# Expert 0 of a mixture of experts: 64 columns as column-tiled F32 pairs in place of 128 columns as split weights

## The chip, the cores and the metric

One core of one Trainium2 chip runs the whole program. The metric is device time in microseconds (us) of one execution; the median of several runs is compared. PE is the matrix engine, PEld its weight load, ACT the scalar engine, DVE the vector engine, POOL the general one, SP the engine that issues nearly all loads here.

## What is computed

A two-layer generator over 256 latent tokens and 256 context tokens, width 1024, all in float32. Each layer mixes tokens with three head groups (gated linear attention, differential softmax attention, neighbourhood attention); layer 0 then has a dense SwiGLU of 2816, layer 1 a mixture of eight experts:

```python
def moe_swiglu(h, w_router, wg, wu, wd):
    logits = (t @ w_router).astype(jnp.float32)
    top_v, top_i = lax.top_k(logits, TOP_K)          # 2 of 8
    top_w = jax.nn.softmax(top_v, axis=-1)
    gates = jnp.sum(jax.nn.one_hot(top_i, N_EXPERTS) * top_w[..., None], axis=1)
    for e in range(N_EXPERTS):
        y = y + gates[:, e:e + 1] * swiglu(t, wg[e], wu[e], wd[e])   # (silu(t wg) * (t wu)) wd
```

An expert's three matrices are 1024 x 3584, 1024 x 3584 and 3584 x 1024, 44.04 MB in all; the eight are 352.3 MB. In layer 1 only the 256 latent tokens pass the experts, 512 token-expert pairs. For the inputs of `setup_inputs()` the router gives the experts 60, 76, 99, 60, 73, 57, 35 and 52 tokens; expert 0 has the first figure.

## The kernel before

Layer 0, then layer 1's mixer with its output projection (four weight tiles, `m2` = 0 to 3, the last matmuls are named `psw`), then the norm, the router, and the experts. An expert works only on its own tokens: one-hot matrices `S` are built from positions (`onehots`), a matmul with `S` gathers the tokens (`gather`, tiles `pga`), and one with its transpose scatters the result back into `xtk` (`scatter_half`, tiles `py`).

Which expert is worked in which place is decided on the chip: `order_experts` sums the tokens per expert (`pcnt`), ranks the experts and permutes positions and gates; `order_index` gives the ranks as integers (`ordi`); `load_order` reads seven of them into SP's registers, since SP addresses the weights of places 1 to 7 by them. Expert 0 is always in place 0 and needs none of it, so that its weights can be loaded ahead.

- Places 0 to 3 are **big**: up to 128 tokens, `expert()`. The hidden 3584 are taken in seven blocks `j` of 512 columns. A block loads two tiles each of gate, up and down, 1.049 MB each, 42 loads an expert. To keep float32 precision every tile is split: ACT rounds it (`eh`, line 804), DVE takes the rest (`el`, line 805), and PE makes three products (lines 151 to 153, and 1151 for down).
- Places 4 to 7 are **small**: up to 64 tokens, `expert_small()`. Weights are used as plain F32, with nothing to split: gate fills PSUM partitions 0 to 63 and up 64 to 127, as a pair (`pgs`, line 1280; `pds` is the down projection, line 1265). Four blocks `j` of 896 columns, each with eight loads of 0.918 MB and four of down (three of 1.049, one of 0.524 MB), 48 loads an expert.

If an expert exceeds its cap, a loop behind a branch (`cv > 0`) runs over all eight experts in two blocks of 128 tokens each, as big experts.

Loads go through a ring of SBUF slots: `slot32(i)` gives load number `i` the next name, and SP's DMA waits until the slot's last reader is done (for a big tile the reader that ends last is `el`). `first` lists the slots of the first 13 loads, `ring` the rest, and `until` the load from which a slot is needed for something else; big experts have ten slots at first, seven from load 42 and five from load 62. `prefetch(i)` issues loads 0 and 1 and their split inside the output projection (`m2` = 1 and 3).

Work that lies between the experts' matmuls is hung on blocks by `plan`: key `(place, j)`, functions run after that block. `add_x` brings the residual stream into `xtk` by 16 transposes (`pxt`). `FILLS` spreads chunks of the modulation vectors (`mod_cols`, 16 matmuls `psmod` and two transposes `ptmod` each) over the earlier stages; its fourth entry stands for the gap at the norm between layer 0's channel mixer and layer 1's mixer. A scheduler then interleaves each engine's instructions, so neighbouring steps of the code mix.

## Time and profile before

| | |
|---|---|
| median of 3 runs | 1952.09 us (1951.88 to 1953.65) |
| profiled execution | 1952.91 us, span 1951.1 us |
| granted PE clock, mean | 0.985 of full speed |
| PE busy | 1814.2 us, 93% |
| DVE, ACT busy | 979.4 us, 758.6 us |
| DMA | 480.05 MB, mean 246 GB/s |
| chain that ended last | PE 72%, DMA 16%, DVE 7%, ACT 3% |

The span is the stretch of the profile from the first to the last instruction; the execution's own time is 1.8 us longer. The page's 40 slices are of 48.8 us. The experts begin in slice 20 and take up the second half of the program; 352.3 of the 480 MB are moved there.

### The profile page before, as it was taken

To read this page: it belongs to the slowest core of one execution; us is meant where nothing else is said; L and a number is where in the kernel's file an instruction comes from. 1 tells how busy PE (TensorE), PEld (TensorE's weight loads), DVE (VectorE), ACT (ScalarE), POOL (GpSimd) and SP (SyncE) were. 2 spreads that over 40 slices of the span, in tenths; PEclk is the share of its full clock that TensorE was granted. 3 is DMA by queue.
4 is the path that set the end of the run, shared out by engine and by line. 5 is a ranking of instruction groups with operands and counts; after the bars stand their busy time and mean duration, and the time that the engine had idled before them with its cause. 6 is when DMAs were issued, how large, how long until landed. Compare 5 with 4: busy or idle time off the path is not lost.

```text
span 1951.1 us, 23538 instructions
## 1 busy us (share of the span) xinstructions
PE 1814.2 (93%) x9280; PEld 1267.4 (65%) x9280; DVE 979.4 (50%) x1294; ACT 758.6 (39%) x965; POOL 46.6 (2%) x75
## 2 busy tenths in 40 slices
PE   7998999999999998999999999999999988787886
PEld 4755766778887876767778778888786333232332
DVE  5474555533333345765669788888985201010101
ACT  4424455422212224344657677767664100000001
POOL 1030000000000000120000000000000000000000
PEclk9999999999999999999989999999999899999999
DMA  9665232343234244564289798999998999999996
GB/s 287 224 179 146 71 129 88 99 145 106 82 108 151 87 132 136 162 161 141 66 306 355 264 320 316 353 327 354 350 353 321 394 410 411 410 410 409 410 410 258
DMA packets 255778, 480.05 MB, mean 246 GB/s; under 512 B 11630, under 2 KB 141996, under 8 KB 249516
## 3 DMA queue, kind: packets, MB, share of 16 engines
q1 hardware_dynamic: 253152, 474.19, 67.8%
q0 software_dynamic: 1312, 2.62, 0.9%
q8 instruction: 75, 1.23, 0.3%
q10 hardware_dynamic: 1196, 1.66, 0.3%
q14 instruction: 43, 0.35, 0.0%
HBM read 477.39 MB, written 1.05 MB: 245 GB/s over the span
## 4 chain that ended last, share of the span: by engine, by line
PE 72%; DMA 16%; DVE 7%; ACT 3%; issue 2%; SPq 0%; POOL 0%; DVEq 0%; ACTq 0%; POOLq 0%
DMA e<-in_w_moe_up_dram 11%; PE pd L1151 8%; PE pgs L1280 3%; DMA e<-in_w_moe_down_dram 3%; PE pu L152 3%; PE pg L151 3%; PE pu L153 3%; PE pg L152 3%; PE pu L151 3%; PE pg L153 3%; PE pds L1265 2%; PE psg L151 2%; PE psg L152 2%; PE psg L153 2%; PE psu L152 2%; PE psu L151 2%
## 5 line engine op out<-in xcount | busy, mean ns | idle before, releaser
L805 DVE TENSOR_TENSOR el<-e,eh 128x2048 fp32r<-128x2048 f32 (+1 forms) x173 | 375.5, 2190 | 50.5 <-ACT eh L804 49.7
L804 ACT ACTIVATE eh<-e 128x2048 fp32r<-128x2048 f32 (+1 forms) x173 | 316.7, 1838 | 94.1 <-PE pu L153 31.8
L1280 PE MATMUL pgs<-e,xs 128*64 128x448 f32 x1024 | 222.8, 552 | 51.3 <-DMA e<-in_w_moe_up_dram 51.3
L144 ACT ACTIVATE wh<-w 128x2048 fp32r<-128x2048 f32 (+2 forms) x70 | 125.3, 1791 | 208.4 <-issue 80.0
L1280 PEld LDWEIGHTS pgs<-e,xs 128*64 128x64 f32 x1024 | 75.1, 138 | 191.9 <-issue 98.7
L145 DVE TENSOR_TENSOR wl<-w,wh 128x2048 fp32r<-128x2048 f32 (+2 forms) x70 | 149.7, 2138 | 98.3 <-ACT wh L144 98.3
L1291 DVE TENSOR_TENSOR es<-es,pgs 64x448 f32<-64x448 f32 x32 | 19.9, 622 | 297.9 <-ACT es L1290 297.9
L1290 ACT ACTIVATE es<-pgs 64x448 f32<-64x448 f32 x32 | 17.2, 537 | 300.6 <-PE pgs L1280 290.3
L1265 PE MATMUL pds<-e,gts 128*64 128x512 f32 x448 | 111.4, 606 | 2.5 <-DMA e<-in_w_moe_down_dram 1.7
L151 PE MATMUL pg<-eh,xeH 128*128 128x512 f32 x224 | 89.9, 402 | 0.6 <-ACT eh L804 0.6
L152 PE MATMUL pg<-el,xeH 128*128 128x512 f32 x224 | 90.0, 402 | 0.0
L151 PE MATMUL psp<-hH,wh 128*128 128x512 f32 (+1 forms) x224 | 86.4, 388 | 3.4 <-ACT hH L276 3.3
L153 PE MATMUL pg<-eh,xeL 128*128 128x512 f32 x224 | 88.9, 397 | 0.0
L152 PE MATMUL pu<-el,xeH 128*128 128x512 f32 x224 | 88.2, 394 | 0.7 <-DVE el L805 0.6
L151 PE MATMUL pu<-eh,xeH 128*128 128x512 f32 x224 | 88.8, 396 | 0.0
L151 PE MATMUL psq<-wh,hH 128*128 128x256 f32 x304 | 88.4, 291 | 0.0
L153 PE MATMUL pu<-eh,xeL 128*128 128x512 f32 x224 | 87.7, 391 | 0.0
L152 PE MATMUL psq<-wl,hH 128*128 128x256 f32 x304 | 87.6, 288 | 0.0
L153 PE MATMUL psq<-wh,hL 128*128 128x256 f32 x304 | 87.3, 287 | 0.0
L152 PE MATMUL psp<-hL,wh 128*128 128x512 f32 (+1 forms) x224 | 85.6, 382 | 0.0
L153 PE MATMUL psp<-hH,wl 128*128 128x512 f32 (+1 forms) x224 | 85.2, 381 | 0.0
L1151 PE MATMUL pd<-eh,gth 128*128 128x512 f32 x224 | 71.2, 400 | 2.6 <-ACT eh L804 2.4
(504 smaller groups left out, 3445.8 us busy)
## 6 DMA issues: line engine op xcount, KB each, us to landing
...
```

Source lines behind the costliest of these rows:

```text
L144: act(wh[:, :m], w32[:, :m], AF.Copy)
L145: tt(wl[:, :m], w32[:, :m], f32(wh[:, :m]), ALU.subtract)
L151: mm(ps, lhsT=sh, rhs=mh, start=first, stop=False)
L152: mm(ps, lhsT=sh, rhs=ml, start=False, stop=False)
L153: mm(ps, lhsT=sl, rhs=mh, start=False, stop=last)
L804: act(h3[:, b], w[:, b], AF.Copy)
L805: tt(l3[:, b], w[:, b], f32(h3[:, b]), ALU.subtract)
L1151: mm(pds[o], lhsT=gt[sh][:, q, :], rhs=w[mh][:, k, o * 512:(o + 1) * 512], start=a and j == 0 and q == 0, stop=z and j == NJ - 1 and q == 3)
L1265: mm(pd[0][H * o:H * o + H, :], lhsT=gt[:, q, :], rhs=w[:, k, o * 512:(o + 1) * 512], start=j == 0 and q == 0, stop=j == NB - 1 and q == F ...
L1280: mm(ps[H * o:H * o + H, b, 0:HB], lhsT=xv[:, kk, :], rhs=ws[o][:, k, b * HB:(b + 1) * HB], start=kk == 0, stop=kk == KD - 1, skip_group_c ...
L1290: act(gv, ps[0:H, b, 0:HB], AF.Silu)
L1291: tt(gv, gv, ps[H:P, b, 0:HB], ALU.mult)
```

## The change

Expert 0, in place 0, is worked as a small expert.

- `CAPS` and the new `SMALL` give place 0 a cap of 64. Its 64 gathered columns `x0` lie in the free half of `xT`, and its tail is that of a small expert.
- `prefetch()` runs once, at `m2` = 3, and issues seven plain loads (`EARLY`) without a split; eight more ring slots follow (`w` to `y`), 15 in all. `until` takes `xt` away at load 24, `mh`, `ml`, `ch` and `cl` at load 30 (big experts need them for split weights), `xh` and `xl` at 68 and `y` at 84. The slot `xc` is gone; `xm` joins the ring after block 0 of place 3, not after block 0 of place 4.
- `plan` has the order of the experts one block earlier, `load_order` with it; `add_x` and the gather of place 1 after block 2 of place 0. `add_x` now copies, since it writes `xtk` first, and the scatter of place 0 adds.
- Every split is one ACT and one DVE instruction (before, the first eight tiles had two).
- `FILLS`: one chunk earlier in layer 0, and two chunks of the layer-1 vectors in the norm gap. `scores()` puts both query tiles of a context head into one bank (layer 0 only).

```diff
@@ -28,12 +28,14 @@
 NE = 8
 EPS = 1e-6
 PRI = 1
-FILLS = "21011010111002110010110011100|11|11100021101|00|2101101110212121110|2".split("|")
-PF = (1, 3)
+FILLS = "21011010111101110010110011100|11|11100021101|11|2101101110111121110|2".split("|")
+NFIRST = 100
+EARLY = ["r0", "r1", "r2", "mh", "ml", "mh", "ml"]
 NBIG = 4
+SMALL = (0, 4, 5, 6, 7)
 FB = 896
 FK = FB // 128
-CAPS = [P] * NBIG + [P // 2] * (NE - NBIG)
+CAPS = [P // 2 if e in SMALL else P for e in range(NE)]
...
     def scores(name, q, k, W, q0, k0):
-        ps = [bank(psc, name) for _ in range(2)]
-        for m in range(2):
-            r = slice(64 * m, 64 * m + 64)
-            mm(ps[m][:, :W], lhsT=q[r, q0:q0 + P], rhs=k[r, k0:k0 + W], start=True, stop=True)
-        return ps
+        n = NT // W
+        while True:
+            ps = [bank(psc, name) for _ in range(2)]
+            for i in range(n):
+                for m in range(2):
+                    r = slice(64 * m, 64 * m + 64)
+                    mm(ps[m][:, i * W:(i + 1) * W], lhsT=q[r, q0:q0 + P], rhs=k[r, k0:k0 + W], start=True, stop=True)
+                q0 += P
+            for i in range(n):
+                yield [p[:, i * W:(i + 1) * W] for p in ps]
...
+                    ps = next(pairs)
...
-            if l == 1 and m2 in PF:
-                prefetch(PF.index(m2))
+            if l == 1 and m2 == 3:
+                prefetch()
...
     def convert(i, w32, dram, kk, n, pl):
...
-        w = w32 if len(w32.shape) == 3 else w32.rearrange("p (b n) -> p b n", n=256)
-        if len(w32.shape) == 3:
...
-        else:
-            nc.sync.dma_start(w32.rearrange("p (k n) -> p k n", n=n), dram)
-        st = 4 if i < 8 else (2 if i in (NE * 42 - 2, NE * 42 - 1) else 8)
+        w = w32.rearrange("p (b n) -> p b n", n=256)
+        nc.sync.dma_start(w32.rearrange("p (k n) -> p k n", n=n), dram)
+        st = 8
         h3 = wh.rearrange("p (b n) -> p b n", n=256)
         l3 = wl.rearrange("p (b n) -> p b n", n=256)
...
-    def prefetch(i):
+    def gu_cols(w_ap, c, j):
+        return w_ap[c * 256:(c + 1) * 256, j * FB:(j + 1) * FB].rearrange("(k p) n -> p k n", p=P)
+
+    def prefetch():
         nonlocal mpr
-        if i == 0:
-            mpr = pool("mpr", 2, side="right")
-        ready[i] = convert(i, ring_tile(f"r{i}"), wm_g[0, 0, i * 512:(i + 1) * 512, 0:512].rearrange("(k p) n -> p k n", p=P), 4, 512, mpr)
+        mpr = pool("mpr", 2, side="right")
+        for i, nm in enumerate(EARLY):
+            w32 = ring_tile(nm) if nm[0] == "r" else mpr.tile([P, 2048], F32, tag="w" + nm[1], name="e32")
+            nc.sync.dma_start(w32[:, :2 * FB].rearrange("p (k n) -> p k n", n=FB), gu_cols((wm_g, wm_u)[i % 2][0, 0], i // 2, 0))
+            ready[i] = w32
 
...
-             "xc": lambda: xT[:, :, NL:NT]}
-    first = ["r0", "r1", "r2", "w", "c", "r0", "r1", "xh", "xl", "xt", "y", "r2", "xc"]
-    ring = ["w", "c", "r0", "r1", "xh", "xl", "xt", "y", "r2", "xc"]
-    until = {"xc": 36, "xt": 42, "y": 42, "xh": 62, "xl": 62}
+             }
+    ring = ["w", "c", "ch", "cl", "xh", "xl", "xt", "y"] + EARLY
+    until = {"xt": 24, "mh": 30, "ml": 30, "ch": 30, "cl": 30, "xh": 68, "xl": 68, "y": 84}
...
-    def onehots_twice():
-        n = NE - NBIG
+    def onehots_twice(e0=NBIG, e1=NE, pos=posp):
+        n = e1 - e0
         it = tb("iota", tab2, TAB_C)[:, 0:P // 2].rearrange("p (a b n) -> p a b n", a=1, b=1).to_broadcast([P, n, 2, P // 2])
         for t in range(2):
-            tt(S[:, t, NBIG:NE, :].rearrange("p e (d n) -> p e d n", d=2), it,
-               posp[:, t, NBIG:NE].rearrange("p (e a b) -> p e a b", a=1, b=1).to_broadcast([P, n, 2, P // 2]), ALU.is_equal)
-
-    tc.keep_in_program_order(onehots(0, 1, posm))
+            i_ = tt(S[:, t, e0:e1, :].rearrange("p e (d n) -> p e d n", d=2), it,
+               pos[:, t, e0:e1].rearrange("p (e a b) -> p e a b", a=1, b=1).to_broadcast([P, n, 2, P // 2]), ALU.is_equal)
+            if e0 == 0:
+                tc.keep_in_program_order(i_)
+
+    onehots_twice(0, 1, posm)
...
                 for k in range(4):
                     nc.tensor.transpose(pt[:, k * P:(k + 1) * P], xT[:, 4 * q + k, t * P:(t + 1) * P], ident)
                 cs = slice(q * 512, (q + 1) * 512)
-                tt(xtk[:, t, cs], xtk[:, t, cs], pt, ALU.add)
+                copy_bal(xtk[:, t, cs], pt)
...
     def slot32(i):
-        if i < len(first):
-            nm = first[i]
-        else:
+        nm = ring.pop(0)
+        while i < NFIRST and i >= until.get(nm, i + 1):
             nm = ring.pop(0)
-            while i >= until.get(nm, i + 1):
-                nm = ring.pop(0)
-            ring.append(nm)
+        ring.append(nm)
         return slots[nm]() if nm in slots else ring_tile(nm)
...
+            tt(xtk[:, t, cs], xtk[:, t, cs], py, ALU.add)
...
     def load_raw(dram, kk, n):
         i = n_load[0]
         n_load[0] += 1
-        w32 = slot32(i)
-        assert len(w32.shape) == 2
+        w32 = slot32(i) if i not in ready else ready[i]
         wv = w32[:, :kk * n].rearrange("p (k n) -> p k n", n=n)
-        nc.sync.dma_start(wv, dram)
+        if i not in ready:
+            nc.sync.dma_start(wv, dram)
         return wv
...
             if e == NBIG and j == 1:
-                ring.extend(["mh", "ml", "mh", "ml", "ch", "cl", "xm"])
+                ring.extend(["mh", "ml", "mh", "ml", "ch", "cl"])
...
-                ws = [load_raw(w_ap[c * 256:(c + 1) * 256, j * FB:(j + 1) * FB].rearrange("(k p) n -> p k n", p=P), 2, FB)
-                      for w_ap in (wg, wu)]
+                ws = [load_raw(gu_cols(w_ap, c, j), 2, FB) for w_ap in (wg, wu)]
...
     xes = {}
-    x01 = xe_tiles(1)
-    gather_at(0, 1, x01)
+    x0 = xT[:, 6:8, NL:NT].rearrange("p a (b n) -> p a b n", n=P // 2)
+    for a in range(2):
+        pt = bank(pmt, "pga")
+        for b in range(4):
+            for i, (src, t) in enumerate(((htH, 0), (htL, 0), (htH, 1), (htL, 1))):
+                mm(pt[:, b * 64:(b + 1) * 64], lhsT=src[:, t, (4 * a + b) * P:(4 * a + b + 1) * P],
+                   rhs=S[:, t, 0, 0:P // 2], start=i == 0, stop=i == 3)
+        copy_bal(x0[:, a], pt[:, 0:256].rearrange("p (b n) -> p b n", n=P // 2))
+
+    def gather_one():
+        xes[1] = gather_at(1, 1, xe_tiles(1))
...
-    plan = {(0, 1): [order_experts], (0, 2): [order_index, lambda: onehots(1, 1, posp)], (0, 4): [lambda: gather_at(1, 1, x01, P), load_order],
-            (0, 6): [lambda: row_bc(ga2b, lambda k: modT[1][:, 40 + k, 0:1])],
+    plan = {(0, 0): [order_experts], (0, 1): [order_index, load_order, lambda: onehots(1, 1, posp)],
+            (0, 2): [add_x, gather_one], (0, 3): [lambda: row_bc(ga2b, lambda k: modT[1][:, 40 + k, 0:1]), stack_ga2],
             (1, 1): [lambda: onehots(2, 2, posp)], (1, 4): [gather_pair],
-            (2, 3): [add_x], (2, 5): [stack_ga2],
-            (3, 1): [onehots_twice], (3, 4): [gather_rest],
+            (3, 0): [lambda: ring.append("xm")], (3, 1): [onehots_twice], (3, 4): [gather_rest],
             (4, 3): [lambda: row_bc(gfb, lambda k: gfT[:, k:k + 1])]}
...
         hooks = {j: f for (ee, j), f in plan.items() if ee == e}
-        if e >= NBIG:
-            tail = expert_small(xes[NBIG], *ws, e, tail, hooks, squares if e == NE - 1 else None)
+        if e in SMALL:
+            xk = (lambda k: x0[:, k // 4, k % 4]) if e == 0 else (lambda k, o=(e - NBIG) * H: xes[NBIG][:, k, o:o + H])
+            tail = expert_small(xk, *ws, e, tail, hooks, squares if e == NE - 1 else None)
             continue
-        xe, h = (x01, e * P) if e < 2 else (xes[2], (e - 2) * P)
+        xe, h = (xes[1], 0) if e < 2 else (xes[2], (e - 2) * P)
```

On SP, where the order of the experts is read (`ordi`), before: behind 28 loads of expert 0 (`e` are its tiles), the last ones these.

```order
L796 DMA xT<-in_w_moe_gate_dram 128x4x256 x2
L798 DMA e_8453<-in_w_moe_gate_dram 128x4x512
L798 DMA e_8480<-in_w_moe_up_dram 128x4x512
L798 DMA e_8498<-in_w_moe_up_dram 128x4x512
L798 DMA e_8519<-in_w_moe_down_dram 128x2x1024
L798 DMA e_8537<-in_w_moe_down_dram 128x2x1024
L1053 TENSOR_LOAD ordi
```

On SP after: behind 20 loads of expert 0, the last four of them being the down tiles of block 0. Load 20 is the gate tile of block 2 that follows the seven reads.

```order
L1238 DMA e_8041<-in_w_moe_gate_dram 128x2x896
L1238 DMA e_8043<-in_w_moe_up_dram 128x2x896
L1238 DMA e_8059<-in_w_moe_down_dram 128x2048
L1238 DMA e_8065<-in_w_moe_down_dram 128x2048
L1238 DMA e_8071<-in_w_moe_down_dram 128x2048
L1238 DMA e_8077<-in_w_moe_down_dram 128x1024
L1062 TENSOR_LOAD ordi
```

The reads moved up from behind the 28th of 42 loads to behind the 20th of 48.

On DVE, what leads to `ordi` before, between the splits of expert 0's weights (the last rows):

```order
L805 TENSOR_TENSOR el<-e_8264,eh 128x2048
L1028 TENSOR_TENSOR pw<-perm,gates 128x64 x2
L805 TENSOR_TENSOR el<-e_8282,eh 128x2048
L1029 TENSOR_REDUCE gatp<-pw 128x16
L1128 TENSOR_TENSOR eg<-eg,pu 128x512
L1036 TENSOR_TENSOR pw<-perm,tab_7068 128x64
L1040 TENSOR_TENSOR pw<-perm,tab_7068 128x64
L1037 TENSOR_REDUCE o<-pw 128x8
L1041 TENSOR_REDUCE base<-pw 128x8
L1038 TENSOR_SCALAR o<-o 128x8
L978 TENSOR_TENSOR S<-tab_7068,posp 128x2x128
L1039 CAST ordi<-o 128x8
```

On DVE after, the same stretch (`es` are the first block's products of gate and up, `S` the one-hots of places 1 and 4 to 7):

```order
L1037 TENSOR_TENSOR pw<-perm,gates 128x64 x2
L985 TENSOR_TENSOR S<-tab_7056,posp 128x2x128
L1291 TENSOR_TENSOR es<-es,pgs 64x448
L1038 TENSOR_REDUCE gatp<-pw 128x16
L985 TENSOR_TENSOR S<-tab_7056,posp 128x2x256
L1045 TENSOR_TENSOR pw<-perm,tab_7056 128x64
L1049 TENSOR_TENSOR pw<-perm,tab_7056 128x64
L1046 TENSOR_REDUCE o<-pw 128x8
L1050 TENSOR_REDUCE base<-pw 128x8
L1047 TENSOR_SCALAR o<-o 128x8
L992 TENSOR_TENSOR S<-tab_7056,posp 128x512
L1048 CAST ordi<-o 128x8
```

No split stands in between any more, but one of the two products `es` (the other is two rows above the piece) and two more one-hot steps do.

On PE at the norm gap before layer 1's mixer, before (`psd` ends layer 0's channel mixer, `psn` is the norm's sum, `psp` the first projection):

```order
L153 MATMUL psd<-gh,wl 128x512
L257 MATMUL psn<-nacc,ones 128x512
L257 MATMUL psn<-sq,ones 128x512
L151 MATMUL psp<-hH,wh 128x256
L151 MATMUL psp<-hH,wh 128x512
L152 MATMUL psp<-hL,wh 128x256
L153 MATMUL psp<-hH,wl 128x256
```

and after:

```order
L233 MATMUL psmod<-wmod,Sz 32x256 x8
L259 MATMUL psn<-nacc,ones 128x512
L233 MATMUL psmod<-wmod,Sz 32x256
L259 MATMUL psn<-sq,ones 128x512
L233 MATMUL psmod<-wmod,Sz 32x256 x3
L217 MATMUL ptmod<-ident,mrow 128x128 x2
L233 MATMUL psmod<-wmod,Sz 32x256 x4
L217 MATMUL ptmod<-ident,mrow 128x128 x2
L153 MATMUL psp<-hH,wh 128x256
```

Two chunks stand around the norm's sums now, ahead of the first projection.

## Rows read from the trace of the kernel before

**Rows 1.** Page, parts 1 and 2: PE's busy us, share; GB/s by slice.

```profile
PE 1814.2 (93%) x9280; PEld 1267.4 (65%) x9280; DVE 979.4 (50%) x1294; ACT 758.6 (39%) x965; POOL 46.6 (2%) x75
...
GB/s 287 224 179 146 71 129 88 99 145 106 82 108 151 87 132 136 162 161 141 66 306 355 264 320 316 353 327 354 350 353 321 394 410 411 410 410 409 410 410 258
```

**Rows 2.** 25-us stretches: length, busy PE, PEld, DVE, ACT, POOL; clock, DMA, GB/s.

```profile
980.00:1005.00 25.00, 22.32 (x100) 17.68 (x100) 10.03 (x25) 10.28 (x17) 0.00 (x0) 0.79 0.71 255
1005.00:1030.00 25.00, 25.00 (x114) 20.49 (x114) 22.86 (x24) 18.29 (x14) 0.00 (x0) 1.00 0.98 361
...
1055.00:1080.00 25.00, 24.22 (x116) 19.62 (x114) 23.30 (x15) 17.26 (x14) 0.00 (x0) 1.00 1.05 387
...
1230.00:1255.00 25.00, 25.00 (x114) 20.39 (x113) 21.30 (x12) 18.75 (x13) 0.00 (x0) 1.00 1.00 375
...
1480.00:1505.00 25.00, 25.00 (x116) 17.50 (x116) 14.52 (x11) 10.51 (x8) 0.00 (x0) 1.00 0.85 299
...
1580.00:1605.00 25.00, 21.19 (x99) 8.22 (x97) 1.73 (x4) 1.62 (x3) 0.00 (x0) 0.93 1.02 410
```

**Rows 3.** Chain that ended last, by time: start us, us, piece, line, count.

```profile
590.62 1.43 PE psmod L231 x24
...
988.23 7.06 PE pga L1096 x32
...
1036.21 5.55 PE pd L1151 x24
1053.28 5.55 PE pd L1151 x24
...
1153.05 4.65 PE pd L1151 x20
...
1295.42 5.57 PE pd L1151 x24
...
1332.07 3.21 PE pd L1151 x14
...
1540.99 6.17 PE pgs L1280 x32
...
1928.70 6.25 PE pds L1265 x28
```

**Rows 4.** Page, part 5: costliest groups, in the columns that the page gives.

```profile
L805 DVE TENSOR_TENSOR el<-e,eh 128x2048 fp32r<-128x2048 f32 (+1 forms) x173 | 375.5, 2190 | 50.5 <-ACT eh L804 49.7
L804 ACT ACTIVATE eh<-e 128x2048 fp32r<-128x2048 f32 (+1 forms) x173 | 316.7, 1838 | 94.1 <-PE pu L153 31.8
L1280 PE MATMUL pgs<-e,xs 128*64 128x448 f32 x1024 | 222.8, 552 | 51.3 <-DMA e<-in_w_moe_up_dram 51.3
...
L1291 DVE TENSOR_TENSOR es<-es,pgs 64x448 f32<-64x448 f32 x32 | 19.9, 622 | 297.9 <-ACT es L1290 297.9
```

**Rows 5.** Waits 940 to 1130 of SP's DMA queue: us in total, times, longest.

```profile
SPq L798 <- DVE el L805: 101.6, 28, 15.0
```

**Rows 6.** Waits 1484 to 1951 of PE.

```profile
PE pgs L1280 <- DMA e<-in_w_moe_up_dram: 51.3, 42, 2.7
```

**Rows 7.** DMA 1450 to 1570 in 40 slices of 3 us, GB/s.

```profile
GB/s 332 376 201 347 414 255 280 367 353 356 380 353 341 337 373 251 240 87 400 346 391 415 389 362 357 358 376 356 400 421 422 406 408 406 405 407 406 420 417 421
```

**Rows 8.** Line 1053: durations in ns, first and last start.

```profile
L1053 SPq TENSOR_LOAD <-ordi x7: 260/262/485, 1044.9 to 1048.5; - x7
```

**Rows 9.** SP in order of time, 1040 to 1052: start us, us.

```profile
1049.17 0.92 SPq L798 DMA_DIRECT2D e<-in_w_moe_gate_dram  x2
```

**Rows 10.** DVE groups 1024 to 1047: busy us, mean ns (first, last).

```profile
L1039 DVE CAST ordi<-o 128x8 int32<-128x8 f32 x1 | 0.2, 166 | 0.0
...
L1010 DVE COPY cnt<-pcnt 128x8 f32<-128x8 f32 x1 | 0.2, 159 | 0.0
```

**Rows 11.** PE in order of time, 736 to 760: start us, us [idle before].

```profile
743.45 1.12 PE L257 MATMUL psn<-sq,ones 128*128 128x512 f32 x2 [1.48 <-ACT sq L248]
747.17 0.90 PE L151 MATMUL psp<-hH,wh 128*128 128x256 f32 x2 [2.60 <-ACT hH L276]
```

More of the change, by code (lines that the diff above doesn't have):

```diff
@@ L553, in diff @@
                       for _ in range(nk // 2)]
+                pairs = scores("pss", dq[:, h], dk[:, h], W, s * NL, k0)
                 for qi in range(2):
@@ L556, in diff @@
                     sm = wk.tile([P, 2], F32, tag="sm", name="sm", bufs=4)
-                    ps = scores("pss", dq[:, h], dk[:, h], W, s * NL + qi * P, k0)
+                    ps = next(pairs)
                     for m in range(2):
@@ L611, in na @@
                         for _ in range(nk // 2)] for _ in range(2)]
+                pairs = scores("psn_", nq[:, hp_], nk_[:, hp_], W, s * NL, k0)
                 for qi in range(2):
-                    ps2 = scores("psn_", nq[:, hp_], nk_[:, hp_], W, s * NL + qi * P, k0)
+                    ps2 = next(pairs)
                     for hh in range(2):
@@ L790, in convert @@
         wl = pl.tile([P, 2048], F32R, tag="wl", name="el")
-        w = w32 if len(w32.shape) == 3 else w32.rearrange("p (b n) -> p b n", n=256)
-        if len(w32.shape) == 3:
-            wv = w.rearrange("p (k h) n -> p k h n", k=kk)
-            dv = dram.rearrange("p k (h n) -> p k h n", n=256)
-            for hh in range(n // 256):
-                nc.sync.dma_start(wv[:, :, hh], dv[:, :, hh])
-        else:
-            nc.sync.dma_start(w32.rearrange("p (k n) -> p k n", n=n), dram)
-        st = 4 if i < 8 else (2 if i in (NE * 42 - 2, NE * 42 - 1) else 8)
+        w = w32.rearrange("p (b n) -> p b n", n=256)
+        nc.sync.dma_start(w32.rearrange("p (k n) -> p k n", n=n), dram)
+        st = 8
         h3 = wh.rearrange("p (b n) -> p b n", n=256)
@@ L1083, in load_e @@
         n_load[0] += 1
-        wh, wl = ready[i] if i in ready else convert(i, slot32(i), dram, kk, n, (mpr, mpr, mpc)[i % 3])
+        wh, wl = convert(i, slot32(i), dram, kk, n, (mpr, mpr, mpc)[i % 3])
         return wh.rearrange("p (k n) -> p k n", n=n), wl.rearrange("p (k n) -> p k n", n=n)
@@ L1103, in gather, with gather_small @@
         return xe
-    def gather_small():
+    def gather_small(xs):
         n = (NE - NBIG) * (P // 2)
-        xs = mp.tile([P, KD, n], F32, tag="xeH1", name="xs")
         for m in range(0, KD, 2):
@@ L1170, in scatter_pre, with scatter_half @@
         return ST, gs, mp2.tile([P, 2, D], F32R, tag="y", name="yHL")
-    def scatter_half(sc, pds, o, first=False):
+    def scatter_half(sc, pds, o):
         ST, gs, yHL = sc
@@ L1183, in scatter_half, with expert @@
             mm(py, lhsT=ST[:, t * P:(t + 1) * P], rhs=yL, start=False, stop=True)
-            if first:
-                copy_bal(xtk[:, t, cs], py)
-            else:
-                tt(xtk[:, t, cs], xtk[:, t, cs], py, ALU.add)
-    def expert(xe, wg, wu, wd, Sf, gate_col, tail, hooks=None, first=False, end=None):
+            tt(xtk[:, t, cs], xtk[:, t, cs], py, ALU.add)
+    def expert(xe, wg, wu, wd, Sf, gate_col, tail, hooks=None, end=None):
         pds = None
@@ L1227, in t1 @@
             for o in range(2):
-                scatter_half(sc, pds, o, first)
+                scatter_half(sc, pds, o)
         return t0, t1
@@ L1241, in expert_small @@
         H = P // 2
-        xv = xs[:, :, (e - NBIG) * H:(e - NBIG + 1) * H]
+        xv = xs
         pd = [None]
@@ L1279, in expert_small @@
                         for o in range(2):
-                            mm(ps[H * o:H * o + H, b, 0:HB], lhsT=xv[:, kk, :], rhs=ws[o][:, k, b * HB:(b + 1) * HB],
+                            mm(ps[H * o:H * o + H, b, 0:HB], lhsT=xv(kk), rhs=ws[o][:, k, b * HB:(b + 1) * HB],
                                start=kk == 0, stop=kk == KD - 1, skip_group_check=True)
@@ L1378, in gather_rest @@
     def gather_rest():
-        xes[NBIG] = gather_small()
+        xes[NBIG] = mp.tile([P, KD, (NE - NBIG) * (P // 2)], F32, tag="xeH1", name="xs")
+        gather_small(xes[NBIG])
     def stack_ga2():
@@ L1398, in hybrid_backbone_kernel @@
         hooks = {j: f for (ee, j), f in plan.items() if ee == e}
-        if e >= NBIG:
-            tail = expert_small(xes[NBIG], *ws, e, tail, hooks, squares if e == NE - 1 else None)
+        if e in SMALL:
+            xk = (lambda k: x0[:, k // 4, k % 4]) if e == 0 else (lambda k, o=(e - NBIG) * H: xes[NBIG][:, k, o:o + H])
+            tail = expert_small(xk, *ws, e, tail, hooks, squares if e == NE - 1 else None)
             continue
-        xe, h = (x01, e * P) if e < 2 else (xes[2], (e - 2) * P)
+        xe, h = (xes[1], 0) if e < 2 else (xes[2], (e - 2) * P)
         xv = (xe[0][:, :, h:h + P], xe[1][:, :, h:h + P])
-        gt_ = gates if e == 0 else gatp
-        tail = expert(xv, *ws, lambda t, e=e: S[:, t, e, :], lambda t, e=e, g=gt_: g[:, t, e:e + 1], tail, hooks, e == 0)
+        tail = expert(xv, *ws, lambda t, e=e: S[:, t, e, :], lambda t, e=e: gatp[:, t, e:e + 1], tail, hooks)
     tail[0]()
```

2 lines of the change are left out of this document (1 added, 1 removed).

## The prediction

> **What bounds the kernel now.** I read the page first: PE is busy 93% of the span, and the GB/s by slice show two halves [rows 1]: below 300 ahead of the experts, 264 and more from there on but for the last. The last eight slices stand at some 410 GB/s: there the small experts wait for loads. The stretches of 25 us split the experts. In a stretch of the big ones (1230) PE works 25.00 of 25.00 us while the DMA moves 375 GB/s; in one of the small ones (1580) PE works 21.19 us and the DMA moves 410 [rows 2]. PE's waits after 1484 are for up tiles, 51.3 us in 42 pieces [rows 6]. The chain shows a big block's pace: the down matmuls start at 1036.21 and 1053.28, so a block takes 17.07 us (17.03 in most of the chain) [rows 3]. Six tiles of 1.049 MB in 17.03 us are 369 GB/s. An expert of 44.04 MB costs PE 7 x 17.03 = 119.2 us as a big one; as a small one, at 410 GB/s, it costs the DMA 107.4 us. PE's own part of a small one is less: 64 gate and up matmuls a block, at the pace of 32 in 6.17 us, and 28 down ones in 6.25 us [rows 3], so 4 x (12.35 + 6.25) = 74 us.
>
> So expert 0 moves from PE to the DMA. But the DMA is what the last four experts wait for too, and it loses time at the start: the 25 us from 980 have 255 GB/s, and SP waits 101.6 us for `el`, that is for a slot, between 940 and 1130 [rows 2, 5]. I therefore draw up when the loads of expert 0 run, and find where the second block of place 1 ends, from where on PE does the same in both kernels. Before, that is the end of the down matmuls that start at 1153.05: 1157.70 [rows 3].
>
> **Expert 0, step by step** (on the clock of before's trace).
>
> 1. Loads 0 to 14 need only slots that earlier work leaves free; by shapes 15 x 0.918 MB, and there are 20 us after the projection for the last eight. I cost them at nothing: they land while norm, router and gather run, until 993.5. If this cover were short by a tile, each would cost 2.2 us (0.918 MB at 410).
> 2. The gather starts at 988.23 and takes 7.06 us for 32 matmuls [rows 3]. With 64 columns instead of 128 I take three quarters, 5.3 (between half and the whole): `x0` is ready at 993.5.
> 3. Block 0: 64 matmuls, 12.35 us at full clock; the granted clock is 0.79 from 980 to 1005 [rows 2], a mean of its two levels of 1.2 and 2.4 GHz, for which I add 2. It ends at 1007.8. Loads 15 to 19 get their slots from its first matmuls and land by about 1010.
> 4. The order: `pcnt` now stands behind these matmuls. Then some 28 DVE steps, the first 159 ns and the last 166, up to 0.7 for the wide one-hots [rows 10], sum 6.3; two `es` of 622 ns [rows 4] stand among them. With 0.4 for `pcnt` that is 7.9: `ordi` at 1015.7. Seven reads go from 1044.9 to 1049.17, where the next load is issued [rows 8, 9]: 4.3 us, so load 20 is issued at 1020.0. I take 2.5 us to its first data: 1022.5. Before, ten slots of loaded tiles covered these 4.3 us. Now nothing does: the DMA is empty from 1010 to 1022.5. That is the one new wait. Behind the reads on SP stand all later loads; PE runs down block 0 and then waits for load 20.
> 5. By then 16 x 0.918 + 3.67 = 18.35 MB of expert 0 are in; 25.7 MB remain, 62.7 us at 410. The ten tiles of place 1 that its second block needs are 10.5 MB, 27.1 us at 387, the best stretch of big tiles [rows 2]. The last lands at 1112.3. ACT 1.84 and DVE 2.19 [rows 4] and its twelve matmuls with what is queued make 7.3: 1119.6. That is 38.1 before 1157.70.
> 6. Place 1 starts without the lead that it had. I allow 2 us of stalls until one is built: 36.1 us are gained.
>
> PE does not undercut this: from 1027.5 its work to the same point, with transposes, gather and tail, is about 86 us, to 1113.7.
>
> **The rest.**
>
> - `add_x` leaves place 2. There the starts at 1295.42 and 1332.07 are two blocks apart [rows 3]: 36.65 in place of 34.06, so 2.6 us gained. In place 0 its 16 transposes lie under the loads.
> - Two chunks of the modulation go to the norm gap, where PE idles 1.48 and 2.60 us [rows 11]. 24 such matmuls take 1.43 us [rows 3], so 16 take 0.95, with two transposes 1.4 a chunk: 2.8 us leave a PE that is full, and I let 0.4 of it delay the first projection. 2.4 us. Bounds: 5 gained, if the shorter gather and the single seven-load `prefetch` (two splits less on ACT and DVE in the projection) also count, and 3 lost, if the chunks delay `hH`'s users and the scores of layer 0 cost a wait.
> - `xm` joins the ring earlier. At the start of place 4 the DMA falls to 251, 240 and 87 GB/s in three slices of 3 us [rows 7]: against 400 that is 1.9 MB, for want of slots, and 299 GB/s in the whole stretch [rows 2]. One slot more is 0.92 MB earlier: 2.3 us, as from there on the loads set the end. Bounds 0 and 4.6, the whole hole.
> - Eight splits become single instructions, the scatter adds instead of copying, the tail of expert 0 becomes a small one: under the loads, nothing; without that cover the four adds of 0.7 us would cost 2.7.
>
> Sum: 36.1 + 2.6 + 2.4 + 2.3 = 43.4 us. The profiled execution took 1952.91 us, 0.04% above the median of 1952.09, so the forecast is **1909.5 us**.
>
> **Where a rule speaks against it.** The small experts' 410 GB/s hold over some 390 us [rows 1]. The Trainium skill ("DMA: Bandwidth & Descriptors", "Where 436 GB/s comes from") says that for transfers between HBM and SBUF the HBM side binds, at about 358 GB/s for a core. The 410 here contradict it, so the trace decides. By its figure, the 25.7 and 10.5 MB of step 5 would take 101.1 us in place of 89.8, and the time would be 1921.
>
> **The rivals.**
>
> - *The lead never comes back.* Big blocks ask for 369 GB/s, and in full stretches the big stage shows 361 to 387 [rows 2]. Place 1 used to enter with full slots; now it enters empty. If big tiles come at 355, a block takes 17.7 in place of 17.03, 0.7 us for each of 19 blocks: 13 us, **1922**. For it: 361 at a DMA share of 0.98. Against it: gathers and transposes stop PE for some 15 us on the way, in which the DMA gains on it.
> - *The loads are better than that.* If the DMA catches up behind the empty 12 us, PE's 1113.7 sets the end, and no stalls follow: 1119.6 - 1113.7 + 2 = 8 us more, **1901**, and 1898 with more gained ahead of the experts. For it: the stretches of 400 and more show in slices [rows 7]. Against it: no long one with big tiles.
> - *The slots of places 1 to 3.* From load 84 on five are left. A slot's turn may last 5/6 of a block, 14.2 us, before PE waits. If without a lead each turn took 16.1 us, a block would take 19.4 and the 19 blocks would eat all 43 us: no change, **1952**, and slower beyond that. Against it: before, places 2 and 3 ran on five slots at 17.03.
> - *It doesn't do what it says.* With 65 tokens or more expert 0 would exceed its cap, and the loop behind the branch would run 16 passes of a big expert, at least 16 x 119 us more: **over 3800**, slower. It has 60.
>
> **How the numbers follow.** Forecast 0.57 (1902 to 1917), no lead 0.25, better loads 0.13, slots 0.04, overflow 0.01. The range takes in the first three with the unknown costs: 2.4 and 2.3 us with their bounds, 0 to 5 us to first data in step 4, 355 to 387 GB/s: 1892 to 1930. 0.2% are 3.9 us, about what a measurement of this kernel can tell from no change. Faster takes the first three cases, 0.95; of the slots, half is no change and half slower: same 0.02, slower 0.03.
>
> **What would show it.** Right: expert 0's first `pgs` near 993; no load in flight from about 1010 to 1022, around the seven reads; the last load of expert 0 landing by about 1096; the second block of place 1 ending near 1120, less what was gained earlier; blocks of 17.03 in places 1 to 3 and none of 18.3 in place 2; a smaller hole at place 4. Wrong: PE waits for `eh` or `el` throughout places 1 to 3 (no lead), or expert 0's loads below 400 GB/s, or the stage ahead of the experts longer than before.

## The result, and the profile after

The changed kernel takes 1922.65 us (median of four runs, 1920.27 to 1924.13) against 1952.66 for the kernel before on the same chip: a ratio of 0.9845, 95% interval 0.9828 to 0.9862, 30 us faster. Forecast were 1909.5 us, 43 us faster, in a range of 1892 to 1930. The profiled execution took 1920.27 us, its span is 1918.5. Between the two profiled executions, then, 32.6 us lie. PE is still busy for 93% of the span; the small experts at the end still run at some 410 GB/s (page, parts 1 and 2, as [rows 1]):

```profile
PE 1781.6 (93%) x9144; PEld 1197.3 (62%) x9144; DVE 881.1 (46%) x1235; ACT 674.2 (35%) x906; POOL 46.7 (2%) x75
...
GB/s 287 232 182 148 72 129 91 88 132 120 83 127 154 85 113 166 169 150 102 123 250 332 384 379 279 344 361 365 363 341 323 411 409 410 411 411 409 409 410 254
```

The chain places the steps; its rows answer to [rows 3]. Columns: start, length, piece.

```profile
982.91 6.89 PE pga L1377 x32
989.81 13.98 PE pgs L1280 x64
...
1058.51 12.23 PE pgs L1280 x64
1075.07 6.16 PE pds L1266 x20
1081.80 2.29 DVE el L808
1098.07 6.17 PE pds L1266 x26
...
1108.73 2.29 DVE el L808
1122.31 3.20 PE pd L1155 x14
1125.94 2.33 PE pd L1155 x10
...
1284.20 3.22 PE pd L1155 x14
...
1301.41 3.22 PE pd L1155 x14
```

The gather of expert 0 starts at 982.91, and the second block of place 1 ends at 1125.94 + 2.33 = 1128.3. I call what lies between the **stretch**: 145.4 us. Before, it went from 988.23 to 1157.70, 169.5 us. So the 32.6 us come apart as follows, beside the terms of the prediction:

| | forecast | measured |
|---|---|---|
| ahead of the gather | 2.4 | 988.23 - 982.91 = 5.3 |
| the stretch | 36.1 | 169.5 - 145.4 = 24.1 |
| from there to place 4 (`add_x` gone) | 2.6 | 338.2 before, 338.5 after: -0.3 |
| start of place 4 (`xm`) | 2.3 | 45.1 before, 40.5 after, to its first full block: 4.7 |
| to the end | 0 | -1.2 |

The stretch is 12 us short of the forecast. It was forecast from the loads, and the loads came nearly as drawn up. GB/s in 40 slices of 4.5 us from 950 to 1130:

```profile
GB/s 346 412 60 0 276 418 412 420 112 0 275 426 319 4 57 416 409 408 421 422 411 390 417 357 374 314 383 404 389 405 424 406 387 388 408 406 402 402 395 344
```

The hole around the seven reads is there, 8 us from 1008 to 1016 (forecast 1010 to 1022.5 on the clock of before, which is 1004.7 to 1017.2 counted from the gather's start here). Behind it the DMA moves a mean of 394 GB/s from 1016.5 to 1107, where step 5 had 36.2 MB in 89.8 us, 403 GB/s; the lowest four slices, 314 to 383, lie around 1060. But PE waited for none of these loads. Its waits from 980 to 1140 (in total, times, longest):

```profile
PE pg L154 <- DVE el L808: 4.0, 2, 2.5
PE ppos L979 <- issue: 1.8, 1, 1.8
PE pgt L1252 <- DVE es L1291: 0.9, 1, 0.9
PE py L1327 <- DVE xT L1319: 0.8, 1, 0.8
PE py L1327 <- DVE xtk L1331: 0.8, 1, 0.8
PE pga L1377 <- ACT htH L974: 0.7, 1, 0.7
PE pxt L1069 <- ACT xtk L291: 0.3, 1, 0.3
```

No load releases any of them. The loads wait for PE instead: the longest waits of SP's DMA queue from 985 to 1090 are for slots that the matmuls of gate and up free.

```profile
SPq L1238 <- PE pgs L1280: 47.9, 9, 21.0
```

The same stretch by stages (length; busy PE, PEld, DVE, ACT, POOL; granted clock, DMA share, GB/s): the end of block 0 with block 1 and the down matmuls of block 0, block 2 with `add_x`, gather and rows, block 3 with the down matmuls of block 2, place 1's first block, expert 0's tail, place 1's second block.

```profile
998.00:1023.60 25.60, 25.60 (x136) 10.07 (x133) 8.39 (x33) 2.69 (x5) 0.00 (x0) 1.00 0.67 266
1023.60:1058.50 34.90, 34.49 (x174) 16.48 (x173) 6.06 (x11) 4.35 (x9) 0.00 (x0) 1.00 1.01 404
1058.50:1081.10 22.60, 21.68 (x106) 8.37 (x105) 2.16 (x5) 4.61 (x5) 0.00 (x0) 0.92 1.00 374
1081.10:1098.00 16.90, 14.40 (x53) 10.18 (x51) 9.52 (x5) 6.39 (x5) 0.00 (x0) 0.90 1.03 406
1098.00:1108.60 10.60, 8.98 (x35) 2.79 (x34) 3.20 (x5) 2.75 (x2) 0.00 (x0) 1.00 1.04 397
1108.60:1128.30 19.70, 18.19 (x82) 14.50 (x82) 18.20 (x12) 12.88 (x9) 0.00 (x0) 1.00 1.03 389
```

In the last row PE waits 1.51 us for a split that comes late in DVE's order. ACT was done with its part at 1098.84, and DVE came to it behind the adds of expert 0's tail:

```profile
1096.92 1.92 ACT L807 ACTIVATE eh<-e 128x2048 fp32r<-128x2048 f32 x1 [4.98 <-DMA e<-in_w_moe_gate_dram]
1108.73 2.28 DVE L808 TENSOR_TENSOR el<-e,eh 128x2048 fp32r<-128x2048 f32 x1
```

PE is busy 34.49 of 34.90 us in the second row. From 1023.6 on it needs 104.7 us, where the prediction had "about 86". What stands there in order of time (start, length):

```profile
1031.93 3.22 PE L1280 MATMUL pgs<-e,xT 128*64 128x448 f32 x14
1035.08 0.44 PE L1069 MATMUL pxt<-ident,xT 128*128 128x128 f32 x2
1035.27 0.31 PE L1102 MATMUL pga<-S,htH 128*128 128x128 f32 x1
1035.51 0.97 PE L1280 MATMUL pgs<-e,xT 128*64 128x448 f32 x2
1036.40 0.55 PE L1102 MATMUL pga<-S,htH 128*128 128x128 f32 x3
```

The scheduler has put the transposes of `add_x` and the gather of place 1 among the column-tiled matmuls. In block 3, where nothing stands between them, 64 take 12.23 us in the chain, 0.19 each. Here 14 take 1035.08 - 1031.93 = 3.15 in place of 2.68, and two take 0.89 in place of 0.38: each run of them costs some 0.5 us more. Why, no run here shows.

### The profile page after: what moved, and what is told of

Read it like the earlier page. It is cut to its first block, busy times and chain, and to the rows that moved or that the text cites. A ratio compares the mean times of both kernels' runs of the same rounds, so it can differ in the third digit from the quotient of the medians.

```text
span 1918.5 us, 23083 instructions
## 1 busy us (share of the span) xinstructions
PE 1781.6 (93%) x9144; PEld 1197.3 (62%) x9144; DVE 881.1 (46%) x1235; ACT 674.2 (35%) x906; POOL 46.7 (2%) x75
## 4 chain that ended last, share of the span: by engine, by line
PE 72%; DMA 15%; DVE 8%; ACT 4%; issue 2%; SPq 0%; POOL 0%; DVEq 0%; ACTq 0%; POOLq 0%
DMA e<-in_w_moe_up_dram 11%; PE pgs L1280 7%; PE pd L1155 6%; PE pds L1266 4%; DMA e<-in_w_moe_down_dram 3%; PE psg L153 2%; PE psg L154 2%; PE psg L155 2%; PE psu L153 2%; PE psu L154 2%; PE psu L155 2%; PE pu L154 2%; PE psd L153 2%; PE pg L154 2%; PE psd L154 2%; PE psd L155 2%
## 5 line engine op out<-in xcount | busy, mean ns | idle before, releaser
L808 DVE TENSOR_TENSOR el<-e,eh 128x2048 fp32r<-128x2048 f32 x126 | 284.9, 2287 | 27.2 <-ACT eh L807 26.7
L807 ACT ACTIVATE eh<-e 128x2048 fp32r<-128x2048 f32 x126 | 240.0, 1917 | 64.7 <-PE pu L155 26.3
L1266 PE MATMUL pds<-e,gts 128*64 128x512 f32 x560 | 139.0, 611 | 2.8 <-DMA e<-in_w_moe_down_dram 1.9
L1266 PEld LDWEIGHTS pds<-e,gts 128*64 128x64 f32 x560 | 41.1, 139 | 75.1 <-issue 61.6
L154 PE MATMUL pg<-el,xeH 128*128 128x512 f32 x168 | 68.0, 405 | 4.0 <-DVE el L808 4.0
L153 PE MATMUL psg<-hH,wh 128*128 128x512 f32 x176 | 70.0, 398 | 1.7 <-ACT hH L278 1.7
L154 PE MATMUL psg<-hL,wh 128*128 128x512 f32 x176 | 69.7, 396 | 0.0
L153 PE MATMUL psd<-gh,wh 128*128 128x512 f32 x176 | 69.6, 396 | 0.0
L155 PE MATMUL psd<-gh,wl 128*128 128x512 f32 x176 | 69.6, 395 | 0.0
L154 PE MATMUL psd<-gl,wh 128*128 128x512 f32 x176 | 69.5, 395 | 0.0
## 6 DMA issues: line engine op xcount, KB each, us to landing
e<-in_w_moe_down_dram SPq DMA_DIRECT2D x102, 1024.0 KB, 17.2
```

Source lines behind the costliest of these rows:

```text
L153: mm(ps, lhsT=sh, rhs=mh, start=first, stop=False)
L154: mm(ps, lhsT=sh, rhs=ml, start=False, stop=False)
L155: mm(ps, lhsT=sl, rhs=mh, start=False, stop=last)
L807: act(h3[:, b], w[:, b], AF.Copy)
L808: tt(l3[:, b], w[:, b], f32(h3[:, b]), ALU.subtract)
L1266: mm(pd[0][H * o:H * o + H, :], lhsT=gt[:, q, :], rhs=w[:, k, o * 512:(o + 1) * 512], start=j == 0 and q == 0, stop=j == NB - 1 and q == F ...
```

## The experiments

The theories: the **PE theory** says that PE's own work and its waits for DVE set the stretch; the **load theory**, which is step 5 of the prediction, that the loads do. All times below of parts are from the profiled execution of each run. I say when ACT's `eh` of place 1's first gate tile starts, which the tile's landing releases; in the changed kernel this is 94.5 us behind the gather's start:

```profile
1077.42 1.91 ACT L807 ACTIVATE eh<-e 128x2048 fp32r<-128x2048 f32 x1 [4.90 <-DMA e<-in_w_moe_gate_dram]
```

**gts_two.** The transposed products `gts` have one buffer. In the changed kernel DVE stood at the copy into it until the down matmuls of block 2 had read it, and the split of place 1 stood behind on DVE:

```profile
1081.26 0.62 DVE L293 COPY gts<-pgt 128x448 f32<-128x448 f32 x1 [5.66 <-PE pds L1266]
1081.80 6.68 DVE L808 TENSOR_TENSOR el<-e,eh 128x2048 fp32r<-128x2048 f32 x3
```

```diff
-            gt = mp2.tile([P, FK, H], F32, tag="gts", name="gts")
+            if e == 0:
+                gt = mp2.tile([P, 4, P], F32, tag="gth", name="gts", bufs=2)
+                gt = gt.rearrange("p q n -> p (q n)")[:, 0:FK * H].rearrange("p (q n) -> p q n", n=H)
+            else:
+                gt = mp2.tile([P, FK, H], F32, tag="gts", name="gts")
```

> Expert 0's transposed products gts get two buffers in place of one (the place of gth, which is free until place 1 works), nothing else. In the changed kernel DVE stands 5.66 us in the copy to gts until the down matmuls of block 2 are done, the split el of place 1's first gate tile stands behind it, and PE waits 2.50 us. PE theory (PE's own work and its waits for DVE set the stretch from the gather's start to the end of place 1's second block, 145.4 us): the copy runs early, the 2.50 us go, and with them the seconds at the lower clock after the wait: 141 to 143 us, total 1918 to 1920. Load theory (the loads of expert 0 and place 1 set the stretch, as in step 5 of the prediction): the tile is there no sooner, 145 us, total 1922 to 1923.

1919.60 us (1917.46 to 1923.47); the stretch 144.0 us. The split came 1.5 us earlier, and PE still waited, 1.83 us, now behind the gate tile itself: ACT's `eh` of it was released by the DMA at 1077.36. The load had been issued when block 3's matmuls had freed its slot:

```profile
1058.24 9.20 PE pgs L1284 x48
1067.44 9.76 DMA e<-in_w_moe_gate_dram
```

At this one place loads and PE come within 2 us of each other. The gain is smaller than the PE theory said, in part for the granted clock: the last 20 down matmuls of block 2 gained by it and place 1's second block lost. The changed kernel, then this run:

```profile
1075.00:1081.14 6.14, 6.14 (x22) 1.73 (x21) 0.49 (x2) 2.98 (x2) 0.00 (x0) 0.72 1.05 392
1108.62:1128.28 19.66, 18.15 (x82) 14.47 (x82) 18.18 (x12) 12.86 (x9) 0.00 (x0) 1.00 1.03 389
```

```profile
1074.74:1079.32 4.58, 4.51 (x21) 1.35 (x21) 0.53 (x4) 1.91 (x1) 0.00 (x0) 1.00 1.04 390
1105.37:1125.87 20.50, 20.29 (x82) 16.18 (x82) 17.68 (x11) 12.87 (x9) 0.00 (x0) 0.87 1.04 403
```

**add_x_twice.**

```diff
-            (0, 2): [add_x, gather_one],
+            (0, 2): [add_x, add_x, gather_one],
```

> add_x runs twice after block 2 of expert 0: 16 more transposes on PE and four more copies, the same values written again. PE theory: the stretch from the gather's start to the end of place 1's second block grows by the price of 16 transposes among column-tiled pairs, 2.6 us for themselves and up to 2 for the breaks: 148 to 150 us, total 1925 to 1927. Load theory: the transposes lie under the loads, 145 to 146 us, total 1922 to 1923.

1925.09 us (1923.23 to 1928.94); the stretch 148.0 us. Sixteen transposes more cost about 2.6 us, and `eh` of place 1's first gate tile starts 94.7 us behind the gather's start, as in the changed kernel: with the tile as early, the stretch is longer. The load theory has no place for that.

**xm_late.** The slot `xm` joins the ring after block 0 of place 4 again.

```diff
-                ring.extend(["mh", "ml", "mh", "ml", "ch", "cl"])
+                ring.extend(["mh", "ml", "mh", "ml", "ch", "cl", "xm"])
...
-            (3, 0): [lambda: ring.append("xm")], (3, 1): [onehots_twice], (3, 4): [gather_rest],
+            (3, 1): [onehots_twice], (3, 4): [gather_rest],
```

> Only the slot xm joins the ring after block 0 of place 4 again. The prediction priced it at 2.3 us (bounds 0 and 4.6); the two traces differ by 4.7 us between the start of place 4 and its first full block. If the slot is all of that: total up by 4 to 5 us, 1927, and the hole of the DMA at the start of place 4 is as it was before. If the other half comes from elsewhere (another state of the ring): up by 2 to 3, 1925.

1924.58 us (1920.74 to 1930.35). The medians differ by less than the runs spread, but the trace shows the place: 45.5 us from the first matmul of place 4 to its first full block, against 40.5 with the slot and 45.1 before. From the first matmul of place 4 to the end of the span the run takes 456.1 us, the changed kernel's two traces 451.7 and 451.1: the slot is worth 4.4 to 5.0 us.

**old_fills.** The string `FILLS` of the kernel before.

```diff
-FILLS = "21011010111101110010110011100|11|11100021101|11|2101101110111121110|2".split("|")
+FILLS = "21011010111002110010110011100|11|11100021101|00|2101101110212121110|2".split("|")
```

> Only FILLS is as before: no chunk in the norm gap, three chunks back in the mixer of layer 1 and one place later in layer 0. The gather of expert 0 starts 5.3 us earlier in the changed kernel than before (988.23 to 982.91); the prediction priced the two chunks at 2.4. If they are worth 2.4, the gather starts at 985.3 and the rest of the 5.3 us belongs to the output projection and the router; if they are worth it all, at 988, total 1927 to 1928.

1930.75 us (1928.11 to 1932.12), 8 us slower, and the gather starts at 992.56, later than before the change. From the first projection of layer 1 to the last norm it takes 225.0 us as before; the changed kernel takes 222.6, and the gap grows by 0.4 there. So the gap's two chunks are worth 2.0 to 2.4 us, as forecast. The rest is in layer 0: PE's 5.0 us wait for a modulation weight is back.

**few_slots.**

```diff
-EARLY = ["r0", "r1", "r2", "mh", "ml", "mh", "ml"]
+EARLY = ["r0", "r1", "r2"]
```

> The ring of expert 0 has eleven slots in place of fifteen, three of them loaded from the last projection on in place of seven; nothing else. Loads 11 to 14 then wait for the first matmuls. Load theory: 3.67 MB come later by the 8 to 9 us that the DMA needs for them, and the end of place 1's second block moves by as much, total about 1931. PE theory as the runs so far leave it (PE has no wait for a load until place 1's first gate tile, which lands just when PE comes to it): the lateness shows there, less what the DMA makes up in the hole around the seven reads (8 us empty in the changed kernel): 0 to 4 us, total 1923 to 1927.

1917.78 us (1916.16 to 1920.29); the stretch 146.8 us. Eleven slots cost at most 2 us in the stretch and nothing that the total shows; from there to place 4 this run takes 337.2 us in place of 338.5. The load theory's 8 to 9 us are not there. But the run does not part the theories: load 15 was issued 18.8 us behind the gather's start in place of 11.9, and behind the hole that lateness was all but gone, `eh` of place 1's first gate tile starting 95.1 us behind it in place of 94.5.

**early_order.**

```diff
+    order_experts()
+    order_index()
+    load_order()
-    plan = {(0, 0): [order_experts], (0, 1): [order_index, load_order, lambda: onehots(1, 1, posp)],
+    plan = {(0, 1): [lambda: onehots(1, 1, posp)],
```

> The order of the experts is worked out and read ahead of expert 0's first block, so that the seven reads stand behind the 15th load in place of the 20th. In the changed kernel the DMA is empty for 8 us around the reads. Load theory (this hole is on the path that sets the end): the end of place 1's second block comes 3 to 8 us sooner, total 1915 to 1920. PE theory: down block 0 covers the hole, PE waits for no load there: 0 to 1 us, total 1922; only PE's wait at place 1's first gate tile can shrink, and that one is DVE's.

1919.75 us (1916.99 to 1920.96); the stretch 145.0 us, no change. This does not part the theories either, since place 1's first gate tile came no sooner: its `eh` starts 95.2 us behind the gather's start, at 983.70.

```profile
1078.91 1.91 ACT L807 ACTIVATE eh<-e 128x2048 fp32r<-128x2048 f32 x1 [4.31 <-DMA e<-in_w_moe_gate_dram]
```

Load 15 now stands behind the reads and is issued 17.6 us behind the gather's start in place of 11.9, and from 1043 to 1050 the DMA falls to 163 GB/s while SP waits for slots that block 2's matmuls free. The hole moved; the loads as a whole did not come earlier. What speaks against the load theory is that no wait of PE is for a load in the changed kernel, and the two runs of `add_x`.

**add_x_early.** The copies go to ACT, the slot `xt` leaves the ring.

```diff
+    for t in range(2):
+        for q in range(2):
+            pt = pdn.tile([P, 512], F32, tag=f"pd{q}", name="pxt")
+            for k in range(4):
+                nc.tensor.transpose(pt[:, k * P:(k + 1) * P], xT[:, 4 * q + k, t * P:(t + 1) * P], ident)
+            act(xtk[:, t, q * 512:(q + 1) * 512], pt, AF.Copy)
     nc.vector.reduce_sum(lg, plt[:, 0:2 * P].rearrange("p (t g s) -> p t s g", g=4, s=32)[:, :, 0:NE, :], axis=AX.X)
...
-            (0, 2): [add_x, gather_one],
+            (0, 2): [gather_one],
```

> The 16 transposes of add_x leave expert 0's third block for the gap behind the last norm's sums, where PE idles 2.1 us; their copies go to ACT, and the slot xt leaves the ring (14 slots). PE theory: the stretch from the gather's start to the end of place 1's second block loses 2.6 us of transposes and up to 2 of breaks among the pairs, 141 to 143 us against 144.7 to 146.5, while the gather may start up to 1 us later; total 1919 to 1921. Load theory: no change but for the missing slot, 1922 to 1925.

1916.41 us (1915.40 to 1916.87); the stretch 141.0 us, 4.4 less than in the changed kernel's first trace, for transposes that themselves took 2.3 from start to next start. The rows show where the 4.4 lie:

```profile
1024.06:1056.87 32.81, 31.65 (x157) 14.72 (x153) 4.68 (x9) 3.16 (x7) 0.00 (x0) 1.00 1.02 415
1073.38:1077.82 4.44, 4.44 (x22) 1.35 (x21) 0.49 (x2) 1.98 (x2) 0.00 (x0) 1.00 1.05 387
```

The stage that the transposes left takes 32.8 us in place of 34.9: 2.1. In the next one 1.8 are gained, nearly all by the last 20 down matmuls of block 2: 4.44 us at a granted clock of 1.00, in place of 6.14 at 0.72. Ahead of block 2 it is 0.5. So not all of the 4.4 is the transposes' own price. The loads followed PE: with a slot less, `eh` of place 1's first gate tile starts at 1075.10, 91.1 us behind the gather's start in place of 94.5.

**three_fixes.** The last edit together with those of gts_two and early_order.

> gts in two buffers, the order of the experts ahead of expert 0, and add_x in the norm gap, together. In the first of these alone PE still waited 1.83 us at place 1, now for the gate tile itself, so loads and PE both bind there. If each only uncovers the other, all three together give what none gives alone: the stretch from the gather to the end of place 1's second block at 138 to 141 us, total 1914 to 1918. If PE alone binds, 140 to 142, the early order adding nothing.

1914.49 us (1913.39 to 1917.73); the stretch 139.7 us. 1.3 less than with `add_x` alone: about what gts_two gave, so that nothing is left for the early order.

**changed_again, old_scores, five_fixes.** In old_fills the norm behind layer 0's mixer began at 362.69, 5 us later than before the change, with the same string: something else in layer 0 cost time. old_scores takes back the packing of the scores alone:

```diff
     def scores(name, q, k, W, q0, k0):
-        n = NT // W
-        while True:
-            ps = [bank(psc, name) for _ in range(2)]
...
+        ps = [bank(psc, name) for _ in range(2)]
+        for m in range(2):
+            r = slice(64 * m, 64 * m + 64)
+            mm(ps[m][:, :W], lhsT=q[r, q0:q0 + P], rhs=k[r, k0:k0 + W], start=True, stop=True)
+        return ps
```

> The changed kernel once more, beside the next two: 1922.65 us, with the gather at 983 to 985, a stretch of 144.7 to 146.5 us to the end of place 1's second block, and PE's waits as in its first trace.

1919.36 us (1918.32 to 1926.06), the stretch 145.2 us, the waits the same. The medians of the changed kernel on two chips are 3 us apart.

> Only scores() is as before: each query tile's scores in banks of their own, not two of a context head in one. With FILLS as before but the new scores the norm behind layer 0's mixer began at 362.69, with both new at 355.10 to 358.30, with both old at 357.89; PE's wait of 5 us for a modulation weight is there in the first and the last and not in the others. If FILLS takes 5 us of wait out and the packing of the scores costs about 4.8 us, the norm begins at 351 to 353 here and the total falls to 1917 to 1919. If the packing is worth nothing and runs differ by such amounts, the norm begins at 355 to 358 and the total stays.

1915.99 us (1912.30 to 1916.95); the norm begins at 348.72. The same two tiles in changed_again, then in old_scores (count, ns, first and last start):

```profile
L538 PE MATMUL pss<-dk,dq x64: 376/534/693, 152.0 to 255.7; 64*128 64x512 f32 x32, 64*128 64x256 f32 x32
L640 PE MATMUL psnv<-nT,nv x48: 379/379/689, 283.1 to 318.2; 128*64 128x256 f32 x48
```

```profile
L535 PE MATMUL pss<-dk,dq x64: 376/534/693, 152.6 to 252.9; 64*128 64x512 f32 x32, 64*128 64x256 f32 x32
L633 PE MATMUL psnv<-nT,nv x48: 379/379/431, 279.6 to 312.0; 128*64 128x256 f32 x48
```

The scores start within 0.6 us of each other; packed they end 2.8 us later, and the neighbourhood heads behind them 6.2. The norm begins 6.5 us later with the packing (355.19 in changed_again), 4.8 with the old string (362.69 to 357.89). It hid most of what the string gives in layer 0: 357.89 (both old) to 348.72 (new string, old scores), 9.2 us. Over the ten traces whose layer 0 is the changed kernel's the norm begins between 355.10 and 358.30, so these sizes hold to some 3 us. Why the packing costs this is not shown.

> The three fixes, with the scores as before, and the row of the gate vector (16 matmuls pbc) worked out ahead of expert 0's first block in place of among its pairs. PE theory: the stretch from the gather to the end of place 1's second block falls from 139.7 by the breaks of pbc, 0.5 to 1.5 us; with the scores' 4.8 us, if they are that, the total is 1908 to 1911; if not, 1913 to 1914.

```diff
+    row_bc(ga2b, lambda k: modT[1][:, 40 + k, 0:1])
+    stack_ga2()
-            (0, 2): [gather_one], (0, 3): [lambda: row_bc(ga2b, lambda k: modT[1][:, 40 + k, 0:1]), stack_ga2],
+            (0, 2): [gather_one],
```

1907.79 us (1903.84 to 1912.74), a ratio of 0.9775 to the kernel before (0.9754 to 0.9795). The stretch stays at 139.7: the rows `pbc`, moved to where the granted clock is 0.51 (981.80 to 985.50), gain nothing. The scores do: the gather starts at 973.41, in three_fixes at 983.39.

**old_places.** From place 1's second block to place 4 the changed kernel gained nothing, though `add_x` had left: a block of places 2 and 3 takes 17.2 us (1284.20 to 1301.41 above) in place of 17.0. Its gate and up matmuls start every 0.234 us there, against 0.228 to 0.230 in most blocks before (24 starts each). The change had moved tiles in SBUF; this run puts them nearly back.

```diff
-    ring = ["w", "c", "ch", "cl", "xh", "xl", "xt", "y"] + EARLY
+    ring = ["w", "ch", "cl", "c", "xh", "xl", "xt", "y"] + EARLY
...
     S = mp.tile([P, 2, NE, P], F32R, name="S")
+    for c_ in "HL":
+        mp.tile([P, KD, 256], F32R, tag=f"xe{c_}1", name=f"xe{c_}")
```

> The changed kernel with its tiles laid out in SBUF nearly as before: the gathered tokens of place 1 below those of places 2 and 3, and the split weights of the pool mpc at their old address; the changed kernel has these in another order. Nothing else (the slots ch and cl are taken before c). From the end of place 1's second block to the first matmul of place 4 the kernel before takes 338.2 us with add_x in it, the changed one 337.2 to 338.6 without it, since a block of places 2 and 3 takes 17.2 in place of 17.0. If where the tiles lie sets this pace: 335 to 336 us, blocks of 17.0 in places 2 and 3, total down by 2.5. If not: 337 to 338.6 again, and the pace stays open.

1920.36 us (1919.70 to 1924.90); 338.6 us, blocks of 17.2. Its theory falls, and the pace stays open. It is not the same in all runs, though: in few_slots a block of places 2 and 3 takes 17.07 us,

```profile
1302.91 3.21 PE pd L1155 x14
...
1319.98 3.21 PE pd L1155 x14
```

and in early_order, three_fixes and five_fixes 17.1. These edits touch when loads are issued or into which slots, not the matmuls of places 2 and 3; by what way they set the pace is not shown.

## Why the prediction was off where it was

- **Steps 1 to 4** held in the main. Block 0 took 14.0 us (14.3 forecast), load 20 was issued 32.2 us behind the gather's start (31.8), and the hole of the DMA came, shorter than forecast. The gather took 6.89 us, not 5.3: 64 columns gained next to nothing over 7.06 for 128. That "the one new wait" would be on the path is wrong: PE worked on block 1 and the down matmuls of block 0 meanwhile, 25.60 of 25.60 us in the first stage above.
- **Step 5** failed, and with it "PE does not undercut this": the 86 us that I gave PE behind down block 0 were 104.7. PE and its waits for DVE, not the loads, set the end of the stretch, and the loads in turn wait for slots that PE frees. Of the 18.7 that the 86 are short, waits make up 6.8 (0.25 + 0.92 + 2.50 + 1.61 + 1.51 in the stages above), all but the first for DVE: 0.92 for the products `es`, 1.61 in expert 0's tail, and 4.0 for a split that stands in DVE's order behind something else, first behind `gts`, then behind the adds of expert 0's tail, although the tile of place 1's second block is there (the rows of `eh` and `el` above). The breaks among the column-tiled matmuls are 4.4: the 64 of block 2 take 16.2 us from start to next start in place of 12.23, and block 1's 28 down ones between them 6.46 in place of 6.01. The granted clock costs 3.9: it is 0.92 and 0.90 in two stages, a mean of 2.4 GHz and of 1.2 GHz behind PE's waits, where the down matmuls of block 2 took 8.0 in place of 6.0 and place 1's first gate 7.5 in place of 5.6. The last 3.6 I take to be plain matmuls and tail priced too low. Only two of these were taken away by a run: the 16 transposes, which with the clock that rose behind them gave 4.4 (2.1 in their own stage), and the buffer of `gts`, which gave 1.4. The rest of the split is read from the trace, not shown by a run. The rival of the better loads had PE set the end, as it did, but with the same 86 us, and so lay on the wrong side at 1901.
- **Step 6** (no lead, 2 us): behind the stretch PE's waits in places 1 to 3 come to 0.7 us (0.6 before), none for a load, so the rival of the lead is not what took the time.
- **Luck.** The time lies in the stated range but above the main case's 1902 to 1917, since step 5 sets the centre. It is where the rival without a lead put it, 1922, for another reason; and 2.9 us more ahead of the gather and 2.4 more at place 4 than forecast made up for part of the 12 that the stretch lacks.
- **Ahead of the experts** 2.4 were forecast, with bounds of 5 and -3, and 5.3 came. The gap was right. In layer 0, costed at nothing, two large effects nearly cancelled: 9.2 us from the string, of them 5 of a wait that [rows 11] did not show, and 6.5 lost to the packing (both to some 3 us).
- **`xm`**: the mechanism right, 2.3 mis-sized: 4.4 to 5.0, about the hole's whole 4.6. One tile's time was too low a price; that the slot lets each later load start earlier too is my reading, which no run tests.
- **`add_x` in place 2**: 2.6 forecast, none seen. The slower pace of 19 blocks takes it, and its cause is open; the layout tried in old_places is not it.

The Trainium skill's figure of 358 GB/s ("DMA: Bandwidth & Descriptors", "Where 436 GB/s comes from") would have given 1921, close to the result, but for another reason: here too the loads came faster, at a mean of 394 from 1016.5 to 1107.
